# Gate and up of two feed-forwards in seven half-size products, and shifted low parts in the splits of 256-column stages

## Chip, cores and metric

The kernel runs on one core of one Trainium2 chip. The metric is the device time of one launch in microseconds: the median of three runs, 1743.22 us before the change (1742.02 to 1744.09).

## The reference, cut to what matters

Two layers work on 256 latent tokens and 256 context tokens of width 1024. Each layer is a feed-forward, a mixer of three kinds of attention, and a second feed-forward; in the last layer the second feed-forward and the mixer's queries run on latent tokens alone. Everything is float32.

```python
D_MODEL, SEQ, CTX_LEN, D_FF, DEPTH = 1024, 256, 256, 2816, 2

def _swiglu(u, w_gate, w_up, w_down):
    return (jax.nn.silu(u @ w_gate) * (u @ w_up)) @ w_down

for l in range(DEPTH):
    # mod_x, mod_c: shift, scale and gate of each part, from silu(c) @ w_ada[l] + b_ada[l]
    h  = h  + 0.5 * g1  * _swiglu(_modulate(_rms_norm(h,  norm_ffn1[l]), sh1,  sc1),  *w_ffn1[l])
    hc = hc + 0.5 * cg1 * _swiglu(_modulate(_rms_norm(hc, norm_ffn1[l]), csh1, csc1), *w_ffn1[l])
    ...  # attention over latent and context tokens, output projection
    h  = h  + 0.5 * g2  * _swiglu(...)      # hc too, but not in the last layer
return _rms_norm(h, norm_final)
```

## The kernel before

Activations lie with the features on the partitions and the 512 tokens (256 latent, `LAT`, then 256 context, `CT`) along the free axis; 1024 features are 8 slices of 128 (`KT`), the inner width 2816 is 22 tiles of 128 (`FT`).

Precision comes from splits. A float32 operand is kept as a high part, rounded to the type that TensorE takes (`F32R`), and a low part, the rest. `wload` (line 126) loads 1024 columns of a weight through SP's DMA queue into one of three `raw` buffers, ACT copies them rounded into the first half of one of four `split` buffers (line 129), and VectorE, called DVE, subtracts to get the low half (line 130). `mm3` (lines 134 to 136) multiplies high by high, high weight by low activation, low weight by high activation into one PSUM bank; each of the three loads its 128 x 128 weights anew.

`ffn` makes one tile of the inner width at a time: `up_one` runs `proj` over the eight slices for gate and for up, 48 matmuls of 512 columns with both kinds of tokens, into the PSUM banks `pg` and `pu` (two of each tag `s` and `t`), and `evac` takes Silu (ACT), the product with up (DVE), and the split into a tile of `G` (ACT, DVE). Tiles go in four parts (`PARTS` = 6, 6, 6, 4). The down product of a part (`down`, banks `pd`) follows the first tile of the next part; that of the last part goes in pieces of 256 columns (`finish`), so that the next normalization can start on one half of the tokens. The last feed-forward, of layer 1, has latent tokens alone, so all its matmuls have 256 columns.

Between the tiles stand `jobs` (`ada_jobs`, `ada_dve`): the modulation vectors of later parts, computed on DVE as sums of products of 1024 columns (line 151), one or two per 128 outputs, from weights that POOL's DMA queue loads into eight `araw` buffers. The tile framework orders each engine's instructions when it compiles, by program order, readiness and a planner's costs; on the chip each engine keeps that order. `FILL` (288 bytes) is an unused tile that sets the addresses of what follows.

In the mixer POOL adds a mask, `maskC`, which is loaded once early, to each head's bias.

Of the kernel before, what the change touches and what calls it, by code (L numbers as in the profile page):

```python
# [23 lines left out]
ABUFS = 8  # L24
# [36 lines left out]
def hybrid_backbone(ctx: ExitStack, tc: tile.TileContext, I, out):  # L61
# [45 lines left out]
    def late_consts_():  # L107
# [3 lines left out]
        late["maskC"] = const("maskC", [128, 2, 256], I["maskC"])  # L111
# [21 lines left out]
    def mm3(ps, wh, wl, xh, xl, first, last):  # L133
        mm(ps, wh, xh, start=first, stop=False)  # L134
        mm(ps, wh, xl, start=False, stop=False)  # L135
        mm(ps, wl, xh, start=False, stop=last)  # L136

    def proj(ps, sp, U, cols, nk=KT, off=0, k0=0, ks=None):
        for k in ks or range(nk):
            o = off + k * 128  # L140
            mm3(ps, sp[:, 0, o:o + 128], sp[:, 1, o:o + 128], U[0][:, k0 + k, cols], U[1][:, k0 + k, cols],
                k == 0, k == nk - 1)


    def ada_dve(l, ft, cb, ntok, pool):
        raw = pool.tile([128, 1024], F32, tag="araw", name="araw", bufs=ABUFS)
# [114 lines left out]
    def first_tiles(pool, csel, U, src):  # L261
# [14 lines left out]
        def a(p, i):  # L276
# [4 lines left out]
            raw = pool.tile([128, 4, 256], F32, tag="araw", name="araw", bufs=ABUFS)  # L281
# [20 lines left out]
        def w(i):  # L302
            raw = raw_load(src(i), 1024)
            if i < 4:
                t = wp.tile([128, 2, 1024], F32R, tag="split", name="split", bufs=4)
                parts = [(t, 0, 1024)]
            else:
                parts = [(pool.tile([128, 2, 512], F32R, tag="G", name="split0", bufs=10), o, 512) for o in (0, 512)]
            for t, o, n in parts:
                act(t[:, 0, :], raw[:, o:o + n], AF.Copy)  # L310
            sps.append((raw, parts))

        def x(i):
            raw, parts = sps[i]
            for t, o, n in parts:
                tt(t[:, 1, :], raw[:, o:o + n], t[:, 0, :].bitcast(F32), ALU.subtract)
# [19 lines left out]
        def m(i, f):  # L336
            t, o, _ = sps[i][1][f // 4 if i >= 4 else 0]
            wh, wl = (t[:, e, f * 128 - o:f * 128 - o + 128] for e in range(2))
# [11 lines left out]
    def ffn(l, w, halves, pool, U, jobs, after, start=None):  # L350
        both = len(halves) == 2
# [13 lines left out]
        def chunk(src, ft):  # L365
            return wload(src[l, :, ft * 1024:(ft + 1) * 1024])

        def evac(pg, pu):
            g = pool.tile([128, 2, TOK], F32R, tag="G", name="G", bufs=10)
            sil = pool.tile([128, TOK], F32, tag="sil", name="sil", bufs=2)  # L370
# [23 lines left out]

        G = {}
        off = [0]

        def down(p0, n, last):
            if not last:
                for d in range(KT):  # L400
                    sp = wload(wd[l, :, off[0]:off[0] + n * 128], n * 128)
                    off[0] += n * 128
                    ps = bank("mm", "pd")
                    for k in range(n):
                        mm3(ps[:, cols], sp[:, 0, k * 128:k * 128 + 128], sp[:, 1, k * 128:k * 128 + 128],
# [3 lines left out]
            else:  # L409
                sps = []  # L410
                for i in range(KT // 2):
                    sps.append(wload(wd[l, :, off[0]:off[0] + n * 256], n * 256))
                    off[0] += n * 256
                def piece(ps, d, h):
                    c = (LAT, CT)[h]
                    o = (d % 2) * n * 128
                    for k in range(n):
                        mm3(ps[:, :256], sps[d // 2][:, 0, o + k * 128:o + k * 128 + 128],
                            sps[d // 2][:, 1, o + k * 128:o + k * 128 + 128],
# [6 lines left out]
        for pi, n in enumerate(PARTS):  # L426
            j = 0
            while j < n:
# [6 lines left out]
                elif ft == 0 and both:  # L435
                    G[0], G[1] = up_two(0)
                    j += 2
# [15 lines left out]
    def mixer(l, pool, U):  # L453
# [4 lines left out]
        perm, rope, maskA, maskC, hsel, qkg, sink, nsink, qg8 = (  # L458
            late[n] for n in ("perm", "rope", "maskA", "maskC", "hsel", "qkg", "sink", "nsink", "qg8"))

        def qk_chunk(i):
            return wload(win[l, :, i * 1024:(i + 1) * 1024])
# [112 lines left out]
        def v_tok(sps, nk, n, dst, t):  # L575
            ps = bank("mm", "pv")
            for k in range(KT):
                s, o = sps[k // nk], (k % nk) * n
                c = slice(t * 128, t * 128 + 128)
                mm(ps[:, :n], U[0][:, k, c], s[:, 0, o:o + n], start=(k == 0), stop=False)  # L580
# [301 lines left out]
def _layout(x, c, ctx, c_ctx, w_ada, b_ada, norm_ffn1, w_ffn1_gate, w_ffn1_up, w_ffn1_down, norm_mix, w_in,  # L882
# [3 lines left out]
    a = {}  # L886
# [62 lines left out]
```

## Time and profile before

| what | value |
|---|---|
| median of three runs | 1743.22 us (1742.02 to 1744.09) |
| the profiled execution's own time | 1742.45 us |
| its span, first to last instruction | 1740.5 us |
| busy PE, DVE, ACT, POOL | 1700.8, 1180.0, 718.5, 165.8 us |
| mean granted clock of TensorE | 0.993 |

The profile is of one execution. PE is TensorE's matmuls, PEld its weight loads, which overlap them. Records of matmuls are pipelined, so a record is longer than the distance from its start to the next one's, and a busy share is not the share of the peak.

### The profile page before, as it was taken

What the parts mean: (1) busy time and instruction counts of PE and PEld (TensorE: products, weight loads), DVE (VectorE), ACT (ScalarE), POOL (GpSimd) and SP (SyncE); (2) the same over time, 40 slices, a digit from 0 to 9 for tenths busy, and PEclk for the clock granted to TensorE, in tenths of its full rate; (3) what the DMA queues carried; (4) which work ended last, traced back from release to release, by engine and by line L of the source; (5) the groups of instructions that cost most, each with busy time, mean ns of one, the idle gap of its engine ahead of it and who ended that gap; (6) DMA issues with size and microseconds to landing.
All of it is one profiled execution on the core that took longest, in us unless ns stands there. A gap on an engine that the chain in (4) does not pass through costs nothing.

```text
span 1740.5 us, 24756 instructions
## 1 busy us (share of the span) xinstructions
PE 1700.8 (98%) x9572; PEld 1477.5 (85%) x9572; DVE 1180.0 (68%) x2031; ACT 718.5 (41%) x1206; POOL 165.8 (10%) x251
## 2 busy tenths in 40 slices
PE   7999999999999999999999999999999999989997
PEld 4888888889888898888888898888888888889997
DVE  5899963447978869983334599934343787965555
ACT  4322222235888653222222442222222577754443
POOL 0311100012102031100000212100000211100000
PEclk9999999999999999999999999999999999989999
DMA  8877643323223247743333288824332333356663
GB/s 330 309 240 243 197 117 84 110 73 115 58 82 85 75 169 238 236 129 89 108 85 109 63 319 277 321 79 115 85 109 86 99 84 102 109 155 182 182 176 113
DMA packets 76693, 258.37 MB, mean 148 GB/s; under 512 B 8944, under 2 KB 11248, under 8 KB 76192
## 3 DMA queue, kind: packets, MB, share of 16 engines
q1 hardware_dynamic: 54096, 176.72, 33.2%
q0 software_dynamic: 21760, 79.38, 14.3%
q8 instruction: 75, 1.23, 0.3%
q10 hardware_dynamic: 720, 0.69, 0.1%
q14 instruction: 42, 0.34, 0.1%
HBM read 250.47 MB, written 1.05 MB: 145 GB/s over the span
## 4 chain that ended last, share of the span: by engine, by line
PE 89%; DVE 4%; ACT 4%; issue 2%; POOL 1%; DMA 1%; POOLq 0%; DVEq 0%; SPq 0%; ACTq 0%
PE pd L135 8%; PE pd L134 8%; PE pd L136 8%; PE pu L134 8%; PE pu L135 8%; PE pu L136 8%; PE pg L134 8%; PE pg L136 8%; PE pg L135 8%; PE pq L136 1%; PE pq L134 1%; PE pq L135 1%; PE pt L679 1%; DVE split L130 1%; PE pv L580 1%
## 5 line engine op out<-in xcount | busy, mean ns | idle before, releaser
L129 ACT ACTIVATE split<-raw 128x1024 fp32r<-128x1024 f32 (+1 forms) x336 | 332.7, 991 | 546.6 <-PE pu L136 223.2
L130 DVE TENSOR_TENSOR split<-raw,split 128x1024 fp32r<-128x1024 f32 (+1 forms) x336 | 383.9, 1143 | 234.1 <-ACT split L129 233.2
L151 DVE SCALAR_TENSOR_TENSOR ascr<-araw,cb 128x1024 f32<-128x1024 f32 x224 | 273.3, 1220 | 9.9 <-ACT cb L804 7.0
L135 PE MATMUL pd<-G,split 128*128 128x512 f32 (+1 forms) x800 | 272.5, 341 | 0.0
L134 PE MATMUL pd<-G,split 128*128 128x512 f32 (+1 forms) x800 | 271.5, 341 | 0.0
L136 PE MATMUL pd<-G,split 128*128 128x512 f32 (+1 forms) x800 | 271.4, 340 | 0.0
L134 PE MATMUL pg<-Uh,split 128*128 128x512 f32 (+1 forms) x712 | 252.4, 355 | 2.1 <-ACT Uh L225 2.1
L136 PE MATMUL pg<-Uh,split 128*128 128x512 f32 (+1 forms) x712 | 252.3, 354 | 0.0
L135 PE MATMUL pg<-Ul,split 128*128 128x512 f32 (+1 forms) x712 | 252.0, 355 | 0.1
L134 PE MATMUL pu<-Uh,split 128*128 128x512 f32 (+1 forms) x712 | 252.1, 354 | 0.0
L135 PE MATMUL pu<-Ul,split 128*128 128x512 f32 (+1 forms) x712 | 251.9, 354 | 0.0
L136 PE MATMUL pu<-Uh,split 128*128 128x512 f32 (+1 forms) x712 | 251.9, 354 | 0.0
L234 DVE SCALAR_TENSOR_TENSOR H<-pd,ada,H 128x256 f32<-128x256 f32 x272 | 123.3, 479 | 106.9 <-PE pd L136 106.8
L135 PEld LDWEIGHTS pd<-G,split 128*128 128x128 f32 x800 | 151.6, 190 | 17.2
L136 PEld LDWEIGHTS pd<-G,split 128*128 128x128 f32 x800 | 151.4, 190 | 16.9
L134 PEld LDWEIGHTS pd<-G,split 128*128 128x128 f32 x800 | 151.1, 189 | 17.3
L134 PEld LDWEIGHTS pg<-Uh,split 128*128 128x128 f32 x712 | 135.4, 190 | 21.0 <-ACT Uh L225 2.6
L135 PEld LDWEIGHTS pg<-Ul,split 128*128 128x128 f32 x712 | 135.4, 190 | 18.6 <-DVE Ul L226 0.3
L136 PEld LDWEIGHTS pu<-Uh,split 128*128 128x128 f32 x712 | 135.2, 190 | 18.5
L136 PEld LDWEIGHTS pg<-Uh,split 128*128 128x128 f32 x712 | 135.2, 190 | 18.4
L134 PEld LDWEIGHTS pu<-Uh,split 128*128 128x128 f32 x712 | 135.3, 190 | 18.3
L135 PEld LDWEIGHTS pu<-Ul,split 128*128 128x128 f32 x712 | 135.0, 190 | 18.4
(199 smaller groups left out, 2412.6 us busy)
## 6 DMA issues: line engine op xcount, KB each, us to landing
araw<-in_w_adaT POOLq DMA_DIRECT2D x128, 512.0 KB, 5.0
raw<-in_w_ffn_gate SPq DMA_DIRECT2D x88, 512.0 KB, 3.8
raw<-in_w_ffn_up SPq DMA_DIRECT2D x88, 512.0 KB, 3.9
raw<-in_w_ffn_down SPq DMA_DIRECT2D x96, 384.0 KB, 3.2
raw<-in_w_in SPq DMA_DIRECT2D x26, 512.0 KB, 3.5
araw<-in_w_ada SPq DMA_DIRECT2D x16, 512.0 KB, 9.9
raw<-in_w_ffn_down SPq DMA_DIRECT2D x16, 512.0 KB, 3.6
raw<-in_w_out SPq DMA_DIRECT2D x16, 512.0 KB, 3.7
```

What stands on the lines that cost most here:

```text
L129: act(sp[:, 0, :n], raw[:, :n], AF.Copy)
L130: tt(sp[:, 1, :n], raw[:, :n], sp[:, 0, :n].bitcast(F32), ALU.subtract)
L134: mm(ps, wh, xh, start=first, stop=False)
L135: mm(ps, wh, xl, start=False, stop=False)
L136: mm(ps, wl, xh, start=False, stop=last)
L151: stt(scr, raw, 1.0, cb[:, t, :], op0=ALU.mult, op1=ALU.mult, accum_out=ada[l][:, ft, t:t + 1])
L234: stt(H[:, d, cols], ps[:, off:off + 256], gate[:, d, half:half + 1], H[:, d, cols], op0=ALU.mult, op1=ALU.add)
L580: mm(ps[:, :n], U[0][:, k, c], s[:, 0, o:o + n], start=(k == 0), stop=False)
L679: nc.tensor.transpose(pt[:, k * 128:(k + 1) * 128], P[t][:, k * 128:(k + 1) * 128], ident)
```

## The change

For the second feed-forward of layer 0 and the first of layer 1 (`FAST`), the tiles from 10 on (`SF`) are made in pairs by `up_fast`. Gate and up of two tiles are a product of 2 x 2 blocks: tokens (latent, context) by features (first four slices, last four), times features by tiles. Instead of eight block products it makes seven, with sums and differences of blocks on both sides (Winograd's form). `forms` makes those of the activations once per feed-forward (`e`, `S`); the second of the two blocks' context part of `U` is written over. Those of the weights are made per pair on DVE from the loaded weights, before the split. Each product, `prod`, is 2 x 4 x 3 matmuls of 256 columns into a bank whose left half is gate and right half is up; two of the seven add to a bank that holds an earlier product.

`split` takes over the second half of `wload`. A split buffer grows from 2048 to 2064 elements, and with `pad` its low half starts 8 elements (32 bytes) further on. `pad` is set where the matmuls have 256 columns: in the seven products, in the last feed-forward, in the pieces of the last down parts, in the output projection where it has one half of the tokens or goes in pieces, and in the query chunks of layer 1.

Room is made for this: `G` has 8 buffers in place of 10 in those two feed-forwards, `araw` 3 in place of 8 in them, and `maskC` is loaded at the start of each mixer.

```diff
-    def wload(src, n=1024):
-        raw = raw_load(src, n)
-        sp = wp.tile([128, 2, 1024], F32R, tag="split", name="split", bufs=4)
-        act(sp[:, 0, :n], raw[:, :n], AF.Copy)
-        tt(sp[:, 1, :n], raw[:, :n], sp[:, 0, :n].bitcast(F32), ALU.subtract)
-        return sp
+    def halves_of(pad):
+        t = wp.tile([128, 2064], F32R, tag="split", name="split", bufs=4)
+        o = 1024 + (8 if pad else 0)
+        return t[:, :1024], t[:, o:o + 1024]
+
+    def wload(src, n=1024, pad=False):
+        return split(raw_load(src, n), n, pad)
+
+    def split(raw, n=1024, pad=False):
+        hi, lo = halves_of(pad)
+        act(hi[:, :n], raw[:, :n], AF.Copy)
+        tt(lo[:, :n], raw[:, :n], hi[:, :n].bitcast(F32), ALU.subtract)
+        return hi, lo
...
+FAST = ((0, 2), (1, 1))
+SF = 10
...
-        late["maskC"] = const("maskC", [128, 2, 256], I["maskC"])
...
+        maskC = pool.tile([128, 2, 256], F32, name="maskC", bufs=1)
+        nc.gpsimd.dma_start(maskC, I["maskC"])
...
+        def forms():
+            LO, HI = slice(0, 4), slice(4, 8)
+            e = {}
+            for a, b in ((1, 0), (0, 0), (1, 1), (0, 1)):
+                t = e[a, b] = pool.tile([128, 2, TOK], F32R, tag="G", name="uu", bufs=gbufs).rearrange(
+                    "p a b -> p (a b)").bitcast(F32)
+                c, k = (LAT, CT)[a], (LO, HI)[b]
+                tt(t.rearrange("p (a b) -> p a b", a=4), U[0][:, k, c].bitcast(F32),
+                                        U[1][:, k, c].bitcast(F32), ALU.add)
+            S = pool.tile([128, 3, 2, 4, 256], F32R, name="S", bufs=1)
+            tt(e[1, 1], e[1, 0], e[1, 1], ALU.add)
+            tt(e[1, 0], e[0, 0], e[1, 0], ALU.subtract)
+            tt(e[0, 0], e[1, 1], e[0, 0], ALU.subtract)
+            tt(e[0, 1], e[0, 1], e[0, 0], ALU.subtract)
+            res = {"11": (U[0][:, LO, LAT], U[1][:, LO, LAT]), "12": (U[0][:, HI, LAT], U[1][:, HI, LAT]),
+                   "22": (U[0][:, HI, CT], U[1][:, HI, CT])}
+            for n, i, j in (("S2", (0, 0), 0), ("S1", (1, 1), 1), ("S3", (1, 0), 2), ("S4", (0, 1), None)):
+                h, lo = (U[0][:, LO, CT], U[1][:, LO, CT]) if j is None else (S[:, j, 0], S[:, j, 1])
+                t = e[i].rearrange("p (a b) -> p a b", a=4)
+                act(h, t, AF.Copy)
+                tt(lo, t, h.bitcast(F32), ALU.subtract)
+                res[n] = (h, lo)
+            return res
+
+        def up_fast(ft, fm):
+            i0 = FAST.index((l, w)), (ft - SF) // 2
+            src = lambda i: I["w_fast"][i0[0], :, (i0[1] * 4 + i) * 1024:(i0[1] * 4 + i + 1) * 1024]
+            b11 = pool.tile([128, 1024], F32, tag="wst", name="b11", bufs=2)
+            nc.sync.dma_start(b11, src(0))
+            b12 = pool.tile([128, 1024], F32, tag="wst", name="b12", bufs=2)
+            nc.sync.dma_start(b12, src(1))
+            b22 = raw_load(src(2), 1024)
+            b21 = raw_load(src(3), 1024)
+            t2 = pool.tile([128, 1024], F32, name="t2", bufs=1)
+            A, X, Y, Z = bank("s", "pa"), bank("t", "px"), bank("s", "py"), bank("t", "pz")
+
+            def prod(ps, w, x, first):
+                sp = split(w, pad=True)
+                xh, xl = fm[x]
+                for i in range(2):
+                    p = ps[:, i * 256:i * 256 + 256]
+                    for k in range(4):
+                        o = i * 512 + k * 128
+                        start = first and i == 0
+                        mm3(p, sp[0][:, o:o + 128], sp[1][:, o:o + 128], xh[:, k], xl[:, k], start and k == 0, k == 3,
+                            not start)
+
+            cc = pool.tile([128, 2, TOK], F32, name="cc", bufs=1)
+            u2, c22 = cc[:, :, LAT], cc[:, :, CT]
+            two = lambda t: t.rearrange("p (a b) -> p a b", a=2)
+            prod(A, b11, "11", True)
+            p1 = pool.tile([128, TOK], F32, tag="sil", name="p1", bufs=3)
+            act(p1, A, AF.Copy)
+            tt(b11, b12, b11, ALU.subtract)
+            tt(t2, b22, b11, ALU.subtract)
+            prod(X, t2, "S2", True)
+            tt(u2, two(X), two(p1), ALU.add)
+            prod(Y, b11, "S1", True)
+            tt(b12, b22, b12, ALU.subtract)
+            prod(Z, b12, "S3", True)
+            u3 = pool.tile([128, TOK], F32, tag="sil", name="u3", bufs=3)
+            tt(two(u3), two(Z), u2, ALU.add)
+            tt(c22, two(Y), two(u3), ALU.add)
+            prod(A, b21, "12", False)
+            sil = pool.tile([128, TOK], F32, tag="sil", name="sil", bufs=3)
+            act(sil[:, LAT], A[:, :256], AF.Silu)
+            tt(sil[:, LAT], sil[:, LAT], A[:, 256:], ALU.mult)
+            tt(t2, t2, b21, ALU.subtract)
+            X = bank("t", "px2")
+            prod(X, t2, "22", True)
+            tt(u3, u3, X, ALU.subtract)
+            act(sil[:, CT], u3[:, :256], AF.Silu)
+            tt(sil[:, CT], sil[:, CT], u3[:, 256:], ALU.mult)
+            prod(Y, b22, "S4", False)
+            tt(u2, two(Y), u2, ALU.add)
+            act(cc[:, 0], cc[:, 0], AF.Silu)
+            tt(cc[:, 0], cc[:, 0], cc[:, 1], ALU.mult)
+            res = []
+            for v in (sil, cc[:, 0]):
+                g = pool.tile([128, 2, TOK], F32R, tag="G", name="G", bufs=gbufs)
+                act(g[:, 0], v, AF.Copy)
+                tt(g[:, 1], v, g[:, 0].bitcast(F32), ALU.subtract)
+                res.append(g)
+            return res
...
+                elif fast and ft >= SF:
+                    fm = fm or forms()
+                    G[ft], G[ft + 1] = up_fast(ft, fm)
+                    j += 2
...
-                jobs = ada_jobs(1, ("shm", "scm"), pool) + ada_jobs(1, ("gm", "sh2", "sc2", "g2"), pool, 1)
+                jobs = ada_jobs(1, ("shm", "scm"), pool, 2, 3)
+                jobs += ada_jobs(1, ("gm", "sh2", "sc2", "g2"), pool, 1, 3)
...
-                jobs = ada_jobs(0, ("g2",), pool) + ada_jobs(1, ("sh1", "sc1", "g1"), pool)
+                jobs = ada_jobs(0, ("g2",), pool, 2, 3)
+                jobs += ada_jobs(1, ("sh1", "sc1", "g1"), pool, 2, 3)
```

## Rows read from the trace of the kernel before

**Rows 1.** The page: the span, and busy time by engine.

```profile
span 1740.5 us, 24756 instructions
...
PE 1700.8 (98%) x9572; PEld 1477.5 (85%) x9572; DVE 1180.0 (68%) x2031; ACT 718.5 (41%) x1206; POOL 165.8 (10%) x251
```

**Rows 2.** Windows: second feed-forward of layer 0, mixer 1, last feed-forward.

```profile
core 0: us, PE busy (x) PEld busy (x) DVE busy (x) ACT busy (x) POOL busy (x), PEclk, DMA share, GB/s
...
638.00:985.00 347.00, 346.70 (x1646) 291.85 (x1646) 210.71 (x323) 99.84 (x130) 20.94 (x38) 1.00 0.48 146
...
1367.00:1536.00 169.00, 160.39 (x1074) 145.46 (x1072) 141.74 (x286) 116.99 (x236) 25.84 (x28) 0.98 0.40 113
1536.00:1730.00 194.00, 193.18 (x1584) 192.83 (x1584) 114.64 (x162) 87.66 (x128) 2.97 (x4) 0.98 0.56 161
```

**Rows 3.** Waits of PE, 630 to 1000: total us, times, longest.

```profile
PE rb L210 <- POOL rs L206: 1.0, 2, 0.5
```

**Rows 4.** Windows inside stretches of 512 columns and of 256, columns as above.

```profile
720.00:960.00 240.00, 240.00 (x1060) 198.72 (x1060) 124.15 (x181) 62.50 (x77) 3.17 (x6) 1.00 0.40 117
1560.00:1720.00 160.00, 160.00 (x1335) 159.90 (x1333) 93.91 (x123) 71.44 (x100) 0.00 (x0) 1.00 0.62 179
```

**Rows 5.** PE's groups by form: count, busy us, mean ns of a record.

```profile
L134 PE MATMUL pg<-Uh,split 128*128 128x512 f32 x472 | 183.6, 389 | 0.0
...
L134 PE MATMUL pg<-Uh,split 128*128 128x256 f32 x240 | 68.8, 288 | 2.1 <-ACT Uh L225 2.1
...
L679 PE MATMUL pt<-ident,P 128*128 128x128 f32 x256 | 36.9, 274 | 0.5 <-ACT P L665 0.5
```

**Rows 6.** Timeline in the last feed-forward: start us, us, what.

```profile
1610.29 0.28 PE L134 MATMUL pg<-Uh,split 128*128 128x256 f32 x1
1610.29 0.19 PEld L135 LDWEIGHTS pg<-Ul,split 128*128 128x128 f32 x1
1610.40 0.28 PE L135 MATMUL pg<-Ul,split 128*128 128x256 f32 x1
```

**Rows 7.** Timeline of PE: first and ninth start of a 256-column stream.

```profile
617.92 0.28 PE L136 MATMUL pd<-Uh,split 128*128 128x256 f32 x1
...
618.86 0.28 PE L135 MATMUL pd<-Ul,split 128*128 128x256 f32 x1
```

**Rows 8.** Timeline of PE: eight transposes merged.

```profile
1507.58 1.03 PE L679 MATMUL pt<-ident,P 128*128 128x128 f32 x8
```

**Rows 9.** Timeline of DVE: two places where it runs back to back.

```profile
700.70 0.68 DVE L372 TENSOR_TENSOR sil<-sil,pu 128x512 f32<-128x512 f32 x1
701.30 0.95 DVE L130 TENSOR_TENSOR split<-raw,split 128x768 fp32r<-128x768 f32 x1
...
1371.78 1.21 DVE L130 TENSOR_TENSOR split<-raw,split 128x1024 fp32r<-128x1024 f32 x1
1372.92 0.47 DVE L226 SCALAR_TENSOR_TENSOR Ul<-t,ada,Uh 128x256 fp32r<-128x256 f32 x1
```

**Rows 10.** Windows: layer 0's second feed-forward before and from tile 10.

```profile
638.00:776.00 138.00, 138.00 (x673) 117.11 (x674) 130.07 (x214) 45.45 (x58) 17.37 (x33) 1.00 0.70 224
776.00:972.00 196.00, 196.00 (x873) 162.52 (x872) 74.38 (x97) 51.08 (x64) 0.00 (x0) 1.00 0.34 97
```

**Rows 11.** ACT's group of weight copies, 776 to 972.

```profile
L129 ACT ACTIVATE split<-raw 128x1024 fp32r<-128x1024 f32 x24 | 25.4, 1058 | 55.6 <-PE pd L136 24.6 <-PE pu L136 23.1 <-issue 7.9
```

**Rows 12.** Windows, the modulation sums (line 151) alone: DVE busy, clock, DMA.

```profile
638.00:776.00 138.00, 78.62 (x128) 1.00 0.70 224
```

**Rows 13.** The tile araw, 630 to 1000: durations, first and last start, landing.

```profile
L151 DVE SCALAR_TENSOR_TENSOR ascr<-araw,cb x64: 1212/1220/1227, 649.0 to 770.9; 128x1024 f32<-128x1024 f32 x64
...
DMA to landing us min/median/max: 3.8/4.6/11.6
```

**Rows 14.** DVE's group of low parts, 776 to 972, with the idle time before.

```profile
L130 DVE TENSOR_TENSOR split<-raw,split 128x1024 fp32r<-128x1024 f32 x25 | 30.6, 1226 | 39.6 <-ACT split L129 39.6
```

**Rows 15.** DMA issues: the mask's load, KB and us to landing.

```profile
maskC<-in_maskC POOLq DMA_DIRECT2D x1, 256.0 KB, 4.9
```

More of the change, by code (lines that the diff above doesn't have):

```diff
@@ L124, in raw_load, with mm3 @@
         return raw
[L126 to L136 removed]
+    def halves_of(pad):
[9 more added lines that the diff above has]
+        return hi, lo
+    def mm3(ps, wh, wl, xh, xl, first, last, go_on=False):
+        mm(ps, wh, xh, start=first, stop=False, skip_group_check=go_on)
+        mm(ps, wh, xl, start=False, stop=False, skip_group_check=go_on)
+        mm(ps, wl, xh, start=False, stop=last, skip_group_check=go_on)
     def proj(ps, sp, U, cols, nk=KT, off=0, k0=0, ks=None):
@@ L304, in w @@
             if i < 4:
-                t = wp.tile([128, 2, 1024], F32R, tag="split", name="split", bufs=4)
-                parts = [(t, 0, 1024)]
-            else:
-                parts = [(pool.tile([128, 2, 512], F32R, tag="G", name="split0", bufs=10), o, 512) for o in (0, 512)]
+                parts = [(halves_of(False), 0, 1024)]
+            else:
+                ts = [pool.tile([128, 2, 512], F32R, tag="G", name="split0", bufs=10) for _ in range(2)]
+                parts = [((t[:, 0], t[:, 1]), o, 512) for t, o in zip(ts, (0, 512))]
             for t, o, n in parts:
-                act(t[:, 0, :], raw[:, o:o + n], AF.Copy)
+                act(t[0], raw[:, o:o + n], AF.Copy)
             sps.append((raw, parts))
@@ L337, in m @@
             t, o, _ = sps[i][1][f // 4 if i >= 4 else 0]
-            wh, wl = (t[:, e, f * 128 - o:f * 128 - o + 128] for e in range(2))
+            wh, wl = (t[e][:, f * 128 - o:f * 128 - o + 128] for e in range(2))
             mm(pss[i], wh, U[0][:, f, :], start=(f == 0), stop=False)
@@ L365, in chunk @@
         def chunk(src, ft):
-            return wload(src[l, :, ft * 1024:(ft + 1) * 1024])
+            return wload(src[l, :, ft * 1024:(ft + 1) * 1024], pad=not both)
         def evac(pg, pu):
-            g = pool.tile([128, 2, TOK], F32R, tag="G", name="G", bufs=10)
-            sil = pool.tile([128, TOK], F32, tag="sil", name="sil", bufs=2)
+            g = pool.tile([128, 2, TOK], F32R, tag="G", name="G", bufs=gbufs)
+            sil = pool.tile([128, TOK], F32, tag="sil", name="sil", bufs=3 if fast else 2)
             act(sil[:, cols], pg[:, cols], AF.Silu)
@@ L400, in down @@
                 for d in range(KT):
-                    sp = wload(wd[l, :, off[0]:off[0] + n * 128], n * 128)
+                    sp = wload(wd[l, :, off[0]:off[0] + n * 128], n * 128, not both)
                     off[0] += n * 128
@@ L457, in mixer @@
         win = I["w_in"]
-        perm, rope, maskA, maskC, hsel, qkg, sink, nsink, qg8 = (
-            late[n] for n in ("perm", "rope", "maskA", "maskC", "hsel", "qkg", "sink", "nsink", "qg8"))
+        perm, rope, maskA, hsel, qkg, sink, nsink, qg8 = (
+            late[n] for n in ("perm", "rope", "maskA", "hsel", "qkg", "sink", "nsink", "qg8"))
+        maskC = pool.tile([128, 2, 256], F32, name="maskC", bufs=1)
+        nc.gpsimd.dma_start(maskC, I["maskC"])
         def qk_chunk(i):
-            return wload(win[l, :, i * 1024:(i + 1) * 1024])
+            return wload(win[l, :, i * 1024:(i + 1) * 1024], pad=i < 8 and not ctxq)
         def rope_lat(x):
@@ L788, in out_proj @@
             else:
-                sps = [wload(I["w_out"][l, :, (4 + i) * 1024:(5 + i) * 1024]) for i in range(4)]
+                sps = [wload(I["w_out"][l, :, (4 + i) * 1024:(5 + i) * 1024], pad=True) for i in range(4)]
                 def piece(ps, d, h):
```

41 lines of the change are left out of this document (25 added, 16 removed).

## The prediction

> **What bounds the kernel.** I read the page's engine line first: PE is busy for 98% of the span, DVE for 68%, ACT for 41% [rows 1]. A busy PE is not yet a PE at its price, so I went by stages next. In the second feed-forward of layer 0 PE has no free time, in the feed-forward of layer 1 that runs on 256 columns only a microsecond, while the mixer of layer 1 leaves gaps [rows 2]; in the whole second feed-forward PE waits 1.0 us for anything but its own work [rows 3]. So what counts is the price of one matmul, start to start. Long stretches give it by their counts: 1060 starts in 240 us make 0.2266 us for a 512-column matmul, 1335 starts in 160 us make 0.120 us for a 256-column one [rows 4]. The records themselves are longer, 389 and 288 ns [rows 5], because they overlap. Two 256-column matmuls thus cost 13 ns more than one of 512: every matmul pays something that does not shrink with its width.
>
> The reader is to see two more things. Each weight load starts with the matmul ahead of it, at 1610.29 both, and the next matmul starts 0.11 to 0.12 us later [rows 6]: at 256 columns load and stream run side by side for their whole length. And the 0.120 is not a law: right after a change of work nine starts lie between 617.92 and 618.86, 0.118 each [rows 7], and eight transposes with 128 columns, in which a weight load is the longer part, stand in a record of 1.03 us whose last one lasts 0.274: (1.03 - 0.274) / 7 = 0.108 us each [rows 5, 8].
>
> **The pairs.** Twelve tiles of each of two feed-forwards, so six pairs each, twelve in all, change form. Before, a pair is 2 tiles x 2 weights x 8 slices x 3 matmuls = 96 of 512 columns: 96 x 0.2266 = 21.75 us. After, it is 7 products x 2 x 4 x 3 = 168 of 256 columns. At 0.120 that is 20.16 us: 1.59 saved, 19.1 us over twelve pairs. Seven eighths of the columns promise 2.72 a pair; 72 more matmuls, each with its fixed part, take 1.13 of it back.
>
> The Trainium skill's page "TensorE: Matmul & The Clock Gate", section "Back-to-back issue gap", gives a warm matmul its columns at 2.4 GHz plus 2.5 ns, which would be 216 and 109 ns and a saving of 28.5 us (an estimate from that page). This trace disagrees by 11 ns at either width, so the sum above goes by the rows.
>
> **The shift.** It moves the low half of a split by 32 bytes against the high half, wherever the stream is 256 columns wide. One load in three (the low part's) then meets the running stream at another offset. No row shows such an offset. Lower bound: each load sheds all it can and a matmul costs 0.109; if only the low part's does, the mean is (2 x 0.120 + 0.109) / 3 = 0.116. Upper bound: it disturbs a pattern that had settled, 0.124, as far above 0.120 as 0.116 lies below. I take 0.117, between the unsettled streams at 0.118 [rows 7], to which I think a broken pattern is nearest, and 0.116. Pairs: 168 x 0.117 = 19.66, so 2.09 saved each, 25.1 us over twelve. Outside them the shift touches 1584 matmuls of the last feed-forward, 3 x 192 in the last down parts of the other three, and some 288 of the output projections that PE runs without gaps: 2448 x 0.003 = 7.3 us.
>
> **What the pairs ask of DVE.** Back to back, a 1024-column DVE instruction costs 1.14 us and a 512-column one 0.60 [rows 9]. Before, a pair has 4 low parts and 4 instructions of 512: 7.0 us. After, 7 low parts and 4 combinations of weights, 11 x 1.14 = 12.5; eight of 512 columns (sums over PSUM, one product, two low parts of G), 4.8; two of 256, some 0.8: 18.2 us against 19.7 of PE. The 12 preparing instructions on the activations come once, 13.7 us. Over the stretch that holds the six pairs and two down parts DVE is now busy for 74 of 196 us [rows 10]; it becomes 74 + 6 x 11.2 + 13.7 = 155 of about 183: 85%. ACT gains some 3.5 us a pair beside copies of 1.06 us [rows 11] and stays below half.
>
> That this room exists is due to the modulation work: its 64 instructions all lie before 776 us, 78.6 us of DVE, the last at 770.9 [rows 12, 13]. In that first stretch DVE is full, 130 of 138 us [rows 10], so the preparation pushes up to 14 us of modulation into the pairs, as work that comes later in the program and fills gaps; 169 of 183 us, 92%, is the worst. Three instead of eight buffers: a load takes 4.6 us to land, its two sums about 2.5; three in flight give one in 2.4 us, 32 in 76 us, where 122 us passed from the first to the last [rows 13]. A sum that waits for its load holds back what stands behind it on DVE, the low parts above all, whose reader is PE; three splits of lead cover that here. I cost it at nothing; with the cover gone it is a wait of some 4.6 us per burst.
>
> At 92% in order, some operand will come late: a DVE instruction of another chain stands ahead of a low part. I take half an instruction, 0.5 us, per pair: 6 us. Bounds: 0, and one uncovered copy and low part a pair, 12 x 2.29 = 27 [rows 11, 14]. Behind the last pair the last G tile needs five steps where four did, and one tile fewer is there to start the down part on: 1 us in each of the two, 2 us. Together 8.
>
> The rest is costed at nothing: the four loads per pair stay four; eight G buffers hold a part's six and the next pair; PSUM banks come free two products ahead. The mask now loads at each mixer's start, 4.9 us to land [rows 15]; behind it on POOL stand its additions to the bias and key exchanges, which heads late in the order need. Without that cover it would be 4.9 us twice.
>
> **Sum.** Against the profiled execution's own 1742.45 us (span 1740.5 [rows 1], 1.95 around it; the median of the runs lies 0.8 higher): -25.1 - 7.3 + 8 = -24.4, so 1718.0; as a median 1719 us.
>
> **Rivals.**
> The shift does nothing. For it: loads and streams at equal offsets run at one steady price at every width, as a fixed cost of changing weights would; against it the 0.118 of rows 7. Time: 1743.2 - 19.1 + 8 = 1732. The same TensorE page, section "Step-by-step: what each phase is for", says this too: "Loading the next tile's weights doesn't steal SBUF read bandwidth from the running matmul." By that rule the shift is worth nothing; the trace has no second offset to say so.
>
> The shift frees more than one load in three. At 0.112, 168 x 0.112 = 18.8 saves 35.2, and 2448 x 0.008 = 19.6: 1743.2 - 54.8 + 8 = 1696; at the bound of 0.109, 1683. For it: transposes reach that. Against it: two loads in three keep their place.
>
> DVE becomes the bound in the pairs, the case on the other side. A low part waits now on average 39.6 / 25 = 1.6 us for its ACT copy [rows 14]. That is idle time, as PE holds the buffers. In a pair four of seven operands are combined first (DVE), then copied (ACT), then subtracted (DVE), on engines that run in a fixed order. DVE has 21.75 - 18.2 = 3.5 us a pair until the saving is gone: it decides from 0.5 us of wait per low part. At 0.8, half of today's, a pair takes 18.2 + 5.6 = 23.8: +24.6 - 7.3, 1760.  Against it: four split buffers let operands be made ahead, and other DVE work is there to fill a wait.
>
> The shift spoils the settled pattern: 0.124 gives 168 x 0.124 = 20.8, saving 11.4, and 2448 x 0.004 = +9.8: with the 8, 1750.
>
> **How the numbers follow.** The forecast 0.40 (1707 to 1726), no effect of the shift 0.27, more than one load 0.12, DVE as the bound 0.13, spoiled pattern 0.06, and 0.02 for sums that cancel. A measurement of this kernel tells 0.2%, 3.5 us, from no change. The first three are faster unless stalls near their bound of 27 meet no effect: 0.78 faster, 0.07 same, 0.15 slower. The range drops the far end of the third case and most of the slow ones: 1699 to 1739.
>
> **What would show it.** After, the pairs' stretch should count 168 starts of 256 columns per pair, at 0.117 where PE does not wait; 0.120 there and in the last feed-forward means that the shift is idle. DVE should be near 85% there, with the 512-column sums among its lines, modulation should end before or shortly behind the first pair, and PE's waits for low parts should stay near 0.5 us a pair. Waits of 2 us, or modulation sums idle on their loads in the first stretch, would make the forecast wrong.

## The result, and the profile after

The changed kernel takes 1764.87 us (median of 4 runs, 1764.22 to 1766.35), the kernel before it took 1742.62 beside it: ratio 1.0128, 95% interval 1.011 to 1.0145. It is slower by 22 us, where 24 us less were forecast, and lies outside the range. The profiled execution has a span of 1762.7 us.

The page of the changed kernel, span and engines, against [rows 1]:

```profile
span 1762.7 us, 26827 instructions
...
PE 1695.1 (96%) x10436; PEld 1500.5 (85%) x10436; DVE 1342.7 (76%) x2211; ACT 773.6 (44%) x1274; POOL 166.2 (9%) x252
```

PE has 864 matmuls more, as the pairs ask, and is busy 5.7 us less, but the share fell from 98% to 96%: 28 us have come in which PE does nothing. PE's waits in the two changed feed-forwards, first 630 to 1010, then 1010 to 1370 (engine, tile, line, what ended the wait: total us, times, longest), against the single microsecond of [rows 3]:

```profile
PE py L144 <- ACT S L427: 5.2, 1, 5.2
PE pa L144 <- ACT split L138: 1.7, 1, 1.7
...
PE pa L144 <- ACT split L138: 10.8, 1, 10.8
PE py L144 <- ACT S L427: 4.5, 1, 4.5
PE py L145 <- DVE S L428: 1.7, 1, 1.7
```

Five waits, 6.9 us in layer 0 and 17.0 in layer 1, all on `pa` and `py`, none of them more than once in a feed-forward: they belong to its first pair, not to pairs as such. The windows of the changed kernel around the two first pairs, and behind them (columns as in [rows 2]):

```profile
782.00:801.00 19.00, 12.11 (x72) 11.47 (x72) 18.81 (x21) 7.18 (x8) 0.00 (x0) 0.73 0.24 74
801.00:980.00 179.00, 179.00 (x1236) 166.47 (x1235) 133.31 (x169) 71.45 (x91) 0.00 (x0) 1.00 0.35 98
...
782.00:980.00 198.00, 191.11 (x1306) 177.94 (x1306) 152.12 (x190) 78.63 (x98) 0.00 (x0) 0.97 0.34 96
...
1153.00:1180.00 27.00, 9.94 (x61) 9.15 (x60) 26.93 (x31) 10.01 (x12) 0.03 (x1) 0.68 0.21 60
1180.00:1360.00 180.00, 180.00 (x1245) 167.60 (x1243) 132.95 (x167) 71.29 (x91) 0.00 (x0) 1.00 0.35 100
```

In the two short windows DVE is full and PE is not; the granted clock means 0.73 and 0.68 there: around the idle time it stood at 0.5, the lower of its two levels, from 789.1 to 799.3 and from 1161.1 to 1178.2, and 256-column matmuls lay 0.214 us apart. Behind them PE has no free time at all and DVE is at 74%, against 38% in [rows 10]. The forecast's 85% held the preparation too: over the whole stretch of the pairs, 782 to 980, DVE is busy for 152.1 us, where 155 were forecast. The amount of its work was right.

The timelines of DVE and PE in the first of these windows say what DVE was full of, and where PE stood (start us, us, line, operation):

```profile
785.40 0.69 DVE L386 TENSOR_TENSOR G<-sil,G 128x512 fp32r<-128x512 f32 x1
786.00 4.62 DVE L415 TENSOR_TENSOR uu<-Uh,Ul 128x1024 f32<-128x1024 f32 x4
790.54 1.22 DVE L418 TENSOR_TENSOR uu<-uu 128x1024 f32<-128x1024 f32 x1
...
798.49 1.22 DVE L428 TENSOR_TENSOR S<-uu,S 128x1024 fp32r<-128x1024 f32 x1
...
787.43 0.27 PE L145 MATMUL pa<-Ul,split 128*128 128x256 f32 x1
792.90 0.58 PE L144 MATMUL py<-S,split 128*128 128x256 f32 x1 [5.20 <-ACT S L427]
```

The preparation of the activations (`forms`) begins in the instant in which the low part of tile 9's G is done, and eleven of its twelve DVE instructions, with one low part of a weight between them, end at 799.7; the twelfth follows at 802.27. PE had finished the pair's first product, over U alone, at 785.5. It went on with two matmuls of another product over U at 787.20 and then stood, in its fixed order, at the first of `py`, which came at 792.90 with the first of the prepared operands. In layer 1 DVE was late already, and two things come together: the chain starts only at 1164.57, and the longest wait, 10.8 us, is not for a prepared operand at all. It is for ACT's copy of a weight, which stands behind ACT's copy of tile 9's G, whose product DVE made at 1163.97, 11 us behind the start of PE's last matmul of that tile (1152.72). In layer 0 it was 1.4 us (783.66 behind 782.28). The rows of layer 1, with DVE's waits for modulation loads between 1010 and 1180 and the loads themselves (count, first and last start); and the first and last sums of layer 0, against [rows 13]:

```profile
1163.97 0.68 DVE L384 TENSOR_TENSOR sil<-sil,pu 128x512 f32<-128x512 f32 x1
...
1164.69 0.63 ACT L385 ACTIVATE G<-sil 128x512 fp32r<-128x512 f32 x1 [4.64 <-DVE sil L384]
...
1165.70 1.05 ACT L138 ACTIVATE split<-raw 128x1024 fp32r<-128x1024 f32 x1
...
DVE ascr L161 <- DMA araw<-in_w_adaT: 14.6, 13, 2.0
...
L158 POOL DMA_DIRECT2D araw<-in_w_adaT x48: 527/527/537, 1010.8 to 1152.5; - x48
...
L161 DVE SCALAR_TENSOR_TENSOR ascr<-araw,cb x64: 1214/1219/1227, 655.3 to 799.6; 128x1024 f32<-128x1024 f32 x64
```

Last, two windows of nothing but 512 columns, one of three steady pairs, and one of 256 columns in the last feed-forward, in the changed kernel:

```profile
150.00:300.00 150.00, 150.00 (x652) 122.22 (x651) 107.93 (x166) 40.07 (x50) 8.60 (x16) 1.00 0.50 153
720.00:780.00 60.00, 60.00 (x261) 48.90 (x261) 58.60 (x94) 15.56 (x18) 6.87 (x13) 1.00 0.66 205
866.00:925.80 59.80, 59.80 (x505) 59.80 (x504) 48.89 (x57) 28.66 (x37) 0.00 (x0) 1.00 0.40 112
...
1620.00:1720.00 100.00, 100.00 (x850) 100.00 (x849) 59.17 (x78) 45.42 (x64) 0.00 (x0) 1.00 0.64 185
```

A window also counts the one or two matmuls that run over its edge. Three pairs take 59.8 us from start to start: 19.93 each, 59.8 / 504 = 0.1187 us a matmul. In the last feed-forward (850 - 2) in 100 us make 0.1179, where [rows 4] gave 0.120. But 512 columns, which the change does not touch, now cost (652 - 2) in 150 us = 0.2308 where [rows 4] gave 0.2266, in layer 0's first feed-forward too, which has no pairs.

### The profile page after: what moved, and what is told of

Its sections match the earlier page's. It is cut to its first block, busy times and chain, and to the rows that moved or that the text cites. A ratio compares the mean times of both kernels' runs of the same rounds, so it can differ in the third digit from the quotient of the medians.

```text
span 1762.7 us, 26827 instructions
## 1 busy us (share of the span) xinstructions
PE 1695.1 (96%) x10436; PEld 1500.5 (85%) x10436; DVE 1342.7 (76%) x2211; ACT 773.6 (44%) x1274; POOL 166.2 (9%) x252
## 3 DMA queue, kind: packets, MB, share of 16 engines
q0 software_dynamic: 21840, 79.65, 14.6%
## 4 chain that ended last, share of the span: by engine, by line
PE 78%; DVE 10%; issue 5%; ACT 4%; DMA 3%; POOL 1%; POOLq 0%; DVEq 0%; SPq 0%; ACTq 0%
PE pd L145 8%; PE pd L146 8%; PE pd L144 8%; PE pg L144 4%; PE pg L146 4%; PE pg L145 4%; PE pu L144 4%; PE pu L146 4%; PE pu L145 4%; DVE ascr L161 2%; DMA araw<-in_w_adaT 2%; DVE split L139 2%; PE pq L144 1%; PE pq L146 1%; PE pq L145 1%
## 5 line engine op out<-in xcount | busy, mean ns | idle before, releaser
L139 DVE TENSOR_TENSOR split<-raw,split 128x1024 fp32r<-128x1024 f32 (+1 forms) x312 | 355.2, 1139 | 136.7 <-ACT split L138 135.4
L144 PE MATMUL pg<-Uh,split 128*128 128x512 f32 (+1 forms) x520 | 178.4, 344 | 2.1 <-ACT Uh L235 2.1
L146 PE MATMUL pg<-Uh,split 128*128 128x512 f32 (+1 forms) x520 | 178.3, 343 | 0.0
L144 PE MATMUL pu<-Uh,split 128*128 128x512 f32 (+1 forms) x520 | 178.0, 342 | 0.0
L146 PE MATMUL pu<-Uh,split 128*128 128x512 f32 (+1 forms) x520 | 177.9, 342 | 0.0
L145 PE MATMUL pg<-Ul,split 128*128 128x512 f32 (+1 forms) x520 | 177.7, 342 | 0.1
L145 PE MATMUL pu<-Ul,split 128*128 128x512 f32 (+1 forms) x520 | 177.4, 341 | 0.0
L203 POOL TENSOR_TENSOR acc<-acc,sq 128x256 f32<-128x256 f32 x40 | 33.9, 848 | 886.0 <-ACT sq L198 885.7
L144 PEld LDWEIGHTS pg<-Uh,split 128*128 128x128 f32 x520 | 98.6, 190 | 14.5 <-ACT Uh L235 2.6
L145 PEld LDWEIGHTS pg<-Ul,split 128*128 128x128 f32 x520 | 98.5, 190 | 12.3 <-DVE Ul L236 0.3
L146 PEld LDWEIGHTS pg<-Uh,split 128*128 128x128 f32 x520 | 98.5, 189 | 12.1
L146 PEld LDWEIGHTS pu<-Uh,split 128*128 128x128 f32 x520 | 98.3, 189 | 12.2
L145 PEld LDWEIGHTS pu<-Ul,split 128*128 128x128 f32 x520 | 98.3, 189 | 11.9
```

The source lines that it names most:

```text
L139: tt(lo[:, :n], raw[:, :n], hi[:, :n].bitcast(F32), ALU.subtract)
L144: mm(ps, wh, xh, start=first, stop=False, skip_group_check=go_on)
L145: mm(ps, wh, xl, start=False, stop=False, skip_group_check=go_on)
L146: mm(ps, wl, xh, start=False, stop=last, skip_group_check=go_on)
L203: (nc.vector if d >= DV else eng).tensor_tensor(accs[half][0], accs[half][0], prev, ALU.add)
```

## The experiments

The first theory after this result had three parts: the preparation comes late at two places; the split buffers, grown by 64 bytes, raise the price of 512 columns; pairs and shift do what they should. The main rival put the 512-column price down to other traffic, of DVE and of the loads, beside PE. The kernel before, timed anew beside the runs, had medians from 1741.56 to 1742.45 us.

**The offsets taken back, pairs kept.**

```
-        t = wp.tile([128, 2064], F32R, tag="split", name="split", bufs=4)
-        o = 1024 + (8 if pad else 0)
+        t = wp.tile([128, 2048], F32R, tag="split", name="split", bufs=4)
+        o = 1024
```

> The changed kernel with its pairs, but split buffers of 2048 elements again and no shift of the low half. Theory (addresses): the 64 bytes by which each split buffer grew put three of four buffers at another offset against the activations, and that made a 512-column matmul 0.231 us in place of 0.2266, in all stages; the shift made a 256-column one 0.118 in place of 0.120. So here 512 columns are back at 0.2266 and 256 columns at 0.120: about 3100 x 4.3 ns = 13 us less, 4460 x 1.7 ns = 8 us more, near 1759 us. Rival (traffic): the pairs' additional DVE and ACT work slows TensorE's reads; then 512 columns stay at 0.231 and the time rises to about 1772 us.

Measured: 1761.51 us (1760.56 to 1762.77), ratio to the kernel before 1.0115 (1.0101 to 1.0129). Windows of this kernel, 512 columns and the last feed-forward:

```profile
150.00:300.00 150.00, 150.00 (x664) 124.24 (x663) 107.33 (x164) 40.13 (x51) 8.06 (x15) 1.00 0.49 151
1620.00:1720.00 100.00, 100.00 (x836) 100.00 (x835) 58.96 (x80) 44.56 (x62) 0.00 (x0) 1.00 0.60 182
```

512 columns are back at 150 / 662 = 0.2266, though DVE, ACT and the loads do in the first window what they did (107 of 150 us, share 0.49): the traffic is not it. 256 columns are back at 100 / 834 = 0.120. The two partly cancel. Over the whole traces, gaps left out, 512-column matmuls on split weights start 231.5 ns apart in the changed kernel and 227.8 here: 3.7 ns on some 3600 of them are 13 us. The 256-column ones go from 119.4 to 120.9, some 8 us on 5400. That leaves 5 us; the runs show 3.4. PE's waits at the first pairs stay (13.9 us on `pa`, 10.3 on `py`).

**The offsets alone, no pairs.** The kernel before with the 2064-element buffers and the shift, and no feed-forward in the list.

```
-ABUFS = 8
+FAST = ()
...
+        t = wp.tile([128, 2064], F32R, tag="split", name="split", bufs=4)
+        o = 1024 + (8 if pad else 0)
```

> The kernel before with the changed split buffers (2064 elements, low half shifted where the changed kernel shifts it) and nothing else: no pairs, eight buffers for modulation weights, ten for G. Theory (addresses): 512-column matmuls at 0.231, 256-column ones at 0.118; some 4300 x 4.3 ns = 18 us more and 2450 x 1.7 ns = 4 us less, near 1756 us. Rival (traffic): without the pairs 512 columns cost 0.2266 and only the shift shows: 1738 us.

Measured: 1754.75 us (1753.47 to 1755.71), ratio 1.0075 (1.0063 to 1.0088): as expected. The same two windows of this kernel:

```profile
150.00:300.00 150.00, 150.00 (x652) 122.22 (x651) 107.90 (x166) 39.72 (x50) 8.62 (x16) 1.00 0.49 153
1620.00:1720.00 100.00, 100.00 (x850) 100.00 (x850) 59.41 (x79) 45.07 (x63) 0.00 (x0) 1.00 0.60 183
```

Both prices of the changed kernel stand in a kernel without pairs. So the offsets, which were to help, lose 13 us by themselves.

**The preparation earlier.** `forms()` is called ahead of tile 7; only the split of S4, which overwrites a part of U, stays ahead of the first pair.

```
+EARLY = 7
...
+                if fast and ft == EARLY:
+                    fm, f4 = forms()
+                    last_form.append(f4)
...
-                    fm = fm or forms()
+                    if last_form:
+                        last_form.pop()()
```

> The changed kernel with the activations' sums, differences and three of the four splits emitted ahead of tile 7 in place of tile 10 (the fourth split overwrites activations that tiles 7 to 9 read, so it stays). Theory (late preparation): the idle of 8 and 19 us at the two first pairs and the half clock behind it come from some 14 us of DVE work that starts only once tile 9's G is written; made early it vanishes in the second feed-forward of layer 0 and mostly in the first of layer 1: near 1740 us. Rival (starved loads): DVE is late because it waits for modulation weights with three buffers; then the wait only moves, and the time stays above 1757 us.

Measured: 1738.24 us (1736.04 to 1741.19), ratio 0.998 (0.9971 to 0.9989): 26.6 us less than the changed kernel, by this move and the order of the engines' instructions that is compiled with it. Its windows over the same places:

```profile
782.00:801.00 19.00, 19.00 (x157) 18.76 (x156) 18.63 (x27) 6.99 (x9) 1.59 (x3) 1.00 0.62 187
...
1150.00:1180.00 30.00, 27.10 (x207) 26.92 (x207) 29.63 (x40) 13.82 (x19) 2.64 (x5) 0.89 0.59 202
```

In layer 0 PE is busy for 19.00 of 19.00 us at full clock. In layer 1 a wait of 2.9 us is left, and the clock dips behind it.

**A map of the offsets.** The kernel before, with the last feed-forward's gate and up weights split into buffers whose high and low halves lie at chosen distances, four loads at each.

```
+PROBE = ((0, 0), (0, 8), (0, 16), (0, 32), (0, 64), (8, 8), (16, 16), (32, 32), (48, 48), (64, 64), (16, 24))
...
+            a, b = PROBE[probe[0] // 4]
```

> The kernel before; in the last feed-forward alone the splits of gate and up lie in buffers of their own, four loads each at eleven offsets of high and low half against the activations (in bytes: 0/0, 0/32, 0/64, 0/128, 0/256, 32/32, 64/64, 128/128, 192/192, 256/256, 64/96). Theory (addresses): the price of a 256-column matmul depends on the offset: 0.120 at 0/0 and, as the 512-column ones in the changed kernel did, again at 256/256; 0.117 to 0.119 in between. Rival (a fixed cost of changing weights): 0.120 at all of them.

Measured (one execution, 1743.21 us): mean distance of starts of 256-column matmuls, worked out from the trace over each group of four loads. The pairs are the bytes by which the high and the low half lie off their first place in the probe's buffers, where the price is that of the kernel before, 120.0.

| high / low | ns | high / low | ns |
|---|---|---|---|
| 0 / 0 | 120.0 | 32 / 32 | 118.4 |
| 0 / 32 | 118.4 | 64 / 64 | 117.8 |
| 0 / 64 | 117.8 | 128 / 128 | 118.7 |
| 0 / 128 | 119.1 | 192 / 192 | 117.85 |
| 0 / 256 | 120.0 | 256 / 256 | 120.1 |
| 64 / 96 | 117.8 | | |

The price comes back at 256 bytes and at no place tried before that, 0 is the dearest of these places for 256 columns, and the low half alone already brings nearly all there is. The 512-column price goes the other way: in the changed kernel the four split buffers in turn cost 226.9, 232.9, 233.0 and 229.2 ns, and their distance to U's place, each grown by 64 bytes, has changed by 256, 192, 128 and 64 bytes. As far as the order of the buffers tells, no run moved the streams by anything but whole multiples of 256 bytes; so whether the distance to the stream counts or the weights' own address was not separated.

**Early and equal offsets**, the first and third edit together.

> The early preparation of e3_forms_early together with the equal offsets of e1_equal_offsets (split buffers of 2048 elements, no shift). If the two causes are independent, as the theories have it, the result is e3 minus what e1 gained on the changed kernel: 1738.2 - 3.4 = 1735 us, with 512 columns at 0.2266 and 256 at 0.120. If TensorE's waits rather than its prices set the pairs' time, nothing is gained: 1738.

Measured: 1735.69 us (1732.05 to 1738.62), ratio 0.9959 (0.9946 to 0.9971). The two edits add up: 3.4 and 26.6 us off 1764.87 make 1734.9.

**Light modulation in the changed kernel.**

```
+            n = 128 if abufs == 3 else 1024
+            nc.gpsimd.dma_start(raw[:, :n], I["w_adaT"][l, :, ft * 1024:ft * 1024 + n])
...
+            stt(scr[:, :n], raw[:, :n], 1.0, cb[:, t, :n], op0=ALU.mult, op1=ALU.mult, ...)
```

> The changed kernel; in the two feed-forwards with pairs each modulation sum and its load take 128 columns in place of 1024, so an eighth (the sums leave out the rest of the products). DVE and the loads are then almost free of modulation. Late preparation (starts behind tile 9's G whatever DVE did before): layer 0's idle of 8 us at the first pair stays, layer 1's falls from 19 to about 8, with less half clock: near 1751 us. Starved loads: both idles vanish, near 1735 us.

Measured: 1755.38 us (1754.9 to 1756.29), ratio 1.0079 (1.0065 to 1.0092), 4 us above the time for late preparation and 20 above that for starved loads. Layer 0's first two pairs stay at 49.6 us (783.0 to 832.6; 50.2 in the changed kernel), layer 1's fall from 59.8 to 49.9. So the late chain costs some 10 us wherever it stands, and the modulation another 10 in layer 1.

**Early, and buffers a multiple of 256 bytes apart.** Early as above; split buffers of 2112 elements, so that all four lie alike against U; the low half 64 bytes off where the stream has 256 columns. To make room, the mask is kept once for both halves of the queries and the product that no one reads (`ascr`) is bfloat16.

```
-        t = wp.tile([128, 2064], F32R, tag="split", name="split", bufs=4)
-        o = 1024 + (8 if pad else 0)
+        t = wp.tile([128, 2112], F32R, tag="split", name="split", bufs=4)
+        o = 1024 + (16 if pad else 0)
```

> Early preparation, and split buffers of 2112 elements, 8448 bytes, a multiple of 256, with the low half 64 bytes further on where the changed kernel shifts it by 32. To make room the mask is kept once for both halves of the queries, which have the same mask, and the unread output of the modulation sums is bfloat16. The probe showed the price to repeat at 256 bytes, so 512 columns should cost 0.2266 and 256 columns 0.118: e5's time less 4460 x 2.2 ns = 10 us, near 1725 us. If the probe's price held only in the last feed-forward, it is e5's time.

Measured: 1726.25 us (1724.38 to 1727.19), ratio 0.9909 (0.9897 to 0.9921). This version beats both kernels. Its windows, 512 columns and three steady pairs:

```profile
150.00:300.00 150.00, 150.00 (x664) 124.20 (x662) 108.02 (x164) 40.21 (x51) 8.62 (x16) 1.00 0.49 153
845.70:905.00 59.30, 59.30 (x505) 59.30 (x504) 48.76 (x57) 28.54 (x37) 0.00 (x0) 1.00 0.37 114
```

512 columns at 0.2266, and 59.3 / 504 = 0.1177 a matmul in the pairs, 19.77 us a pair.

**The same offsets without pairs.** The kernel before with the layout, the shift and the single mask of the last one.

> The kernel before with the split buffers of e7_early_period256 (2112 elements, low half 64 bytes on in 256-column stages, mask kept once) and no pairs. 512 columns at 0.2266, 2450 matmuls of 256 columns at 0.118: 2450 x 2.2 ns = 5 us less than before, 1737 us. If a shift costs elsewhere what it gives, no change.

Measured: 1738.91 us (1737.04 to 1740.28), ratio 0.9984 (0.9975 to 0.9992): the shift outside the pairs is worth 2.7 us. The pairs then bring 1738.91 - 1726.25 = 12.7 us, not the 12 x (21.75 - 19.77) = 23.8 that their steady form gives. Layer 0 has 10.3 of its 11.9 us (from the second part's gate and up, 741.6 to 1000.3 without pairs, 740.8 to 989.2 with them); the other 1.6 go at the start of its last down part, whose first 97 matmuls take 13.2 us with pairs (957.5 to 970.7) and 11.6 without. Layer 1 has 0.7 of its 11.9. Its first two pairs take 46.7 us where two steady ones take 39.6.

**Light modulation with the early preparation**: the kernel of 1726.25 us with the edit of the sixth run.

> The kernel of the eighth run of this study that timed 1726.25 us (activations prepared ahead of tile 7, buffers a multiple of 256 bytes apart, low parts 64 bytes off), but in the two changed feed-forwards each modulation load and sum takes 128 of 1024 columns (it leaves out the rest of those sums). In layer 1 its first two pairs still take 46.7 us of PE where two steady ones take 39.6, and the ordinary tile ahead of them 34.6 where 32.7 is usual: 9.0 us. Theory: DVE is late there because modulation sums stand between the combinations and low parts of the first pair; then these 9.0 us go, PE's 3.1 us wait for cc at the first pair of layer 1 goes, and the time is 1717 (1715 to 1720). Rival: the chain of combinations inside the first pair is late by itself (ACT copy, DVE low part, PSUM), whatever else DVE does: the wait stays at 2 to 3 us with the half clock behind it, 1724 to 1727.

Measured: 1717.64 us (1717.25 to 1718.0), ratio 0.986 (0.9845 to 0.9876), as the theory had it. Layer 1's first two pairs now take 39.6 us, and the window over them shows PE without a gap:

```profile
1150.00:1180.00 30.00, 30.00 (x216) 28.26 (x216) 22.71 (x32) 13.95 (x19) 0.00 (x0) 1.00 0.43 128
```

**Pairs of layer 1 from tile 12**, else as the seventh run.

```
-                elif fast and ft >= SF:
+                elif fast and ft >= SF + 2 * l:
```

> The kernel of the run that timed 1726.25 us, with one difference: in layer 1 pairs begin at tile 12 in place of tile 10 (five pairs, the activations still prepared ahead of tile 7), so that modulation, which ends near 1175 us there, lies mostly ahead of them. Theory that modulation on DVE costs the first two pairs 9.0 us: one pair's saving of 21.75 - 19.79 = 1.96 us is given up and most of the 9.0 us comes back, 1719 to 1721. Rival, the first pair is late wherever it stands: 1726.25 + 2 = 1728, with a wait of PE of 2 to 3 us for cc at tile 12.

Measured: 1726.09 us (1724.7 to 1729.83), ratio 0.9912 (0.9898 to 0.9927): a miss for the theory. Modulation does end early, its last sum starts at 1155.9, but the first pair still takes 24.5 us, and the two tiles that became ordinary again meet late operands themselves: PE's waits between 1060 and 1200 in this kernel:

```profile
PE pu L147 <- DVE split L140: 1.5, 1, 1.5
PE px L145 <- ACT split L139: 1.5, 1, 1.5
PE pd L145 <- DVE H L245: 1.5, 1, 1.5
PE px L147 <- DVE split L140: 1.2, 1, 1.2
```

The rival's time, 1728, is near, but not its wait for `cc`: DVE is late with low parts, wherever the pairs begin.

**Full loads, light sums.** As the seventh run, but each sum reads 128 of the 1024 columns that its load brings.

> The kernel that timed 1726.25 us, with full loads of modulation weights through three buffers, but in the two changed feed-forwards each sum over them reads 128 of 1024 columns (it leaves out the rest of the sums). The run that cut loads and sums alike timed 1717.64, so modulation costs layer 1's first pairs 9 us, either as work of DVE or as loads that come late in three buffers and hold DVE's order. Theory, the work: a sum shrinks from 1.22 to 0.29 us, 64 of them from 78 to 19 us, and the time is 1717 to 1719 even with full loads. Rival, the loads: sums end late still (behind 1120 us, where the cut loads ended at 1063), DVE's waits for araw stay, and the time is 1722 to 1726.

Measured: 1738.36 us (1736.15 to 1741.82), ratio 0.9981 (0.9971 to 0.999), 12 us slower than with full sums: neither theory said so. Waits in this kernel, of DVE from 980 to 1200, then of PE from 600 to 1400:

```profile
DVE ascr L163 <- DMA araw<-in_w_adaT: 55.4, 34, 4.3
...
PE pd L145 <- DVE H L246: 8.1, 2, 7.1
PE pd L145 <- ACT G L387: 4.5, 1, 4.5
```

DVE stands 55.4 us at loads that have not landed, 9.4 in the seventh run. It keeps its order, so the additions into H and the low parts behind a waiting sum come late, and a down part of PE takes 50.3 us (1068.0 to 1118.3) where 33 are usual. The pairs behind it run clean, two in 39.6 us. So fewer columns on DVE did not help while the loads were full. A wait for a load is not dear by itself: with light loads, in the ninth run, DVE stands 22.0 us at them, but the last sum starts at 1062.9 and the pairs meet none of it. The order is compiled anew for each kernel, so the sums stand elsewhere in it (the last starts at 1107.0 here, at 1178.9 in the seventh run); how much of the 12 us is due to that was not separated.

**Two buffers for these loads in place of three**, else as the seventh run.

> The kernel that timed 1726.25 us, with two buffers for the loads of modulation weights in place of three, in both changed feed-forwards. A load lands 4.8 us behind its issue. If the number of buffers delays modulation, two of them bring one load per 3 us or so, the sums of layer 1 end 20 us and more behind the 1179 us of three buffers, more pairs meet them, and the time is 1732 to 1745. If DVE's volume alone sets it, nothing is later than with three: 1726 to 1729.

Measured: 1750.66 us (1746.91 to 1752.08), ratio 1.0045 (1.0029 to 1.0061). The sums of layer 1 end 41 us later than with three:

```profile
L162 DVE SCALAR_TENSOR_TENSOR ascr<-araw,cb x64: 1215/1224/1227, 1012.6 to 1219.8; 128x1024 bf16<-128x1024 f32 x64
```

One buffer fewer costs 24.4 us, and the time lies above the 1732 to 1745 that were expected if the loads set it; the direction is theirs. More than three were not tried.

## Why the prediction was wrong

**The step that failed first** is the sentence that costs the preparation: "The 12 preparing instructions on the activations come once, 13.7 us", counted as DVE time that "pushes up to 14 us of modulation into the pairs". The size was right (twelve instructions of 1.14 us), the place was not asked for. The products over S need a chain of sums, ACT copies and low parts, and the chain starts behind tile 9's G. What is late next is PE, by 6.9 us in layer 0 and, with DVE late, 17.0 in layer 1. The first two pairs take 50.2 us (782.5 to 832.7) and 59.8 (1153.0 to 1212.8) where two steady ones take 39.9: 30.2 us lost against the 8 that were allowed for all stalls. What the waits leave of it, 3.4 and 2.9 us, fits the matmuls at the half clock. Moving the call took 26.6 us back, which shows the cause. The sixth run splits the loss: some 10 us at each place stay with the modulation light, and 10 more in layer 1 are DVE's lateness, which the move took back in large part too; by what, the chain's place or the new order, was not separated. Two things keep the chain behind tile 9, the program order and the G buffers that its operands share; which of them holds alone was not separated.

**The second** is what the sum costed at nothing without naming it: the buffers' growth by 64 bytes. The prediction looked for the price of an offset in the 256-column streams alone; three of four buffers also moved for the 512-column streams, and those became dearer by 3.7 ns on average, 13 us. Without pairs, where more matmuls have 512 columns, the offsets cost 1754.75 - 1741.69 = 13.1 us net of their gain. That the kernel before keeps an unused tile to set addresses was there to be read.

**The third** is "I cost it at nothing" of three buffers for the modulation's loads. In layer 0 that held: DVE waited for no load there. But "one in 2.4 us, 32 in 76 us" was worked out for layer 0, where each load feeds two sums; layer 1 makes its 64 sums from 48 loads. In the changed kernel these go out 3.0 us apart (1010.8 to 1152.5), and DVE waits 13 times for them, 14.6 us in all and 2.0 at most, not the "4.6 us per burst" that were to show the loss of the cover. Light modulation takes 9.5 us off the changed kernel and 8.6 off the best version, and a buffer fewer adds 24.4. The light sums with full loads, slower by 12 us, and the two buffers point to the coming of the loads, which hold DVE's fixed order, rather than to the columns summed; with the order compiled anew in each kernel that is argued, not shown.

**What was right.** A pair in its steady state costs 19.93 us in the changed kernel and 19.77 with the better layout, forecast 19.66 without stalls; inside steady pairs PE waits for nothing, where 0.5 us a pair was allowed. The term "25.1 us over twelve" measured 21.8. That the shift makes 256 columns cheaper holds, 120.0 to 118.4 or 117.8 ns. The Trainium skill's page "TensorE: Matmul & The Clock Gate", section "Step-by-step: what each phase is for", says that a weight load takes no read bandwidth from the running matmul. Taken as a rule on price, as the prediction took it, it would make the map of the offsets flat; the map is not flat, 117.8 to 120.1 ns, though no run shows that read bandwidth is what differs. But "7.3 us" outside the pairs measured 2.7: in the eighth run the price fell by some 2.2 ns (120.0 to 117.8 in the last feed-forward) where 3 were taken, under all of the 2448 matmuls that were counted. That makes 5.4 us; where the other 2.7 went was not found. The 2 us for what comes "Behind the last pair" measured 2.9: the first 97 matmuls of the last down part take 13.2 us (979.0 to 992.2, and again in layer 1) where they took 11.7 and 11.8.

**The rivals.** The time came out where "DVE becomes the bound" had it, 1760, for another reason: DVE is at 74% behind the first pair and no steady pair takes 23.8 us. "The shift spoils" had an effect of the right sign and looked at the wrong width. "More than one load in three" found nothing: with both halves moved 256 columns cost what they cost with the low half moved, 117.8 ns at 64 bytes.

**The sum again**, against the profiled executions (22.2 us between the spans): pairs -21.8, shift outside them -2.7 (as in the eighth run; by the prices in this kernel's own trace it would be nearer 5), first pairs +30.2, 512 columns +13, start of the last down parts +2.9: +21.6. The rest, 1 to 3 us, was not settled.

## What to carry to other kernels

Work that runs once ahead of a new form is priced as a chain: ask what its first reader is, when its operands and its buffers come free, and what the engine behind it does meanwhile; busy shares say nothing on that. A change of a buffer's size moves every buffer behind it: count all matmuls whose weights or streams move, of every width, before one width's gain is booked. And fewer buffers for a background load are a cost at the place where the in-order engine next has something urgent to do.

## What had not been expected of the hardware

The price of a matmul depends on where its weights lie, and comes back at 256 bytes: 120.0 ns at 0 and 117.8 at 64 for 256 columns, but 226.9 ns at 0 and 229 to 233 elsewhere for 512. No one of these places was cheapest for both; the best version here gives each width its own. And around idle times of PE of 5.2 us in layer 0, and of 10.8, 4.5 and 1.7 us close together in layer 1, the granted clock stood at half for 10 and 17 us.
